# Attention fillers and attended tiles: the splits of four attended tiles ahead of the 13th block's softmax, and the fourth group of values ahead of pair 7's projection

## The chip, the cores and the metric

The kernel runs on one core of a Trainium2 chip. The metric is device time in microseconds (us) of one execution. A core has a matrix engine (TensorE, PE in the profile; its weight loads are PEld), a vector engine (DVE), a scalar engine (ACT), GpSimd (POOL) and a queue engine (SP) that issues transfers. Each engine works through its own list of instructions in the order in which the program was written, and semaphores hold an instruction until what it needs is there. Matrix products land in eight PSUM banks; everything else lies in SBUF, here mostly in 41 "pages" of 128 x 1024 float32.

## The reference, cut to what matters

Two layers of a decoder trunk: a short gated convolution with its feed-forward, then dilated attention with its feed-forward, then a last norm. The change lies in the attention of the second layer.

```python
def dilated_attention_mixer(h, w_qkv, w_out, rel_bias):
    qkv = (h @ w_qkv).reshape(bsz, seq, 3, N_HEADS, HEAD_DIM)      # seq 1024, 16 heads x 64
    q, k, v = qkv[:, :, 0], qkv[:, :, 1], qkv[:, :, 2]
    for window, dilation in ((128, 1), (512, 4), (2048, 16)):
        o, l = dilated_branch(q, k, v, rel_bias, window, dilation)   # banded softmax attention
    alpha = jax.nn.softmax(jnp.stack(lses, axis=0), axis=0)
    o = jnp.sum(alpha[..., None] * jnp.stack(outs, axis=0), axis=0)
    return o.reshape(bsz, seq, D_MODEL).astype(h.dtype) @ w_out

x = x + dilated_attention_mixer(rms_norm(x, mix_norm[1]), attn_w_qkv[0], attn_w_out[0], rel_bias)
```

## The kernel before, in words

All large products are made of float32 operands that are split into a high and a low part (`split`, L134 to L146): ACT copies the source into a rounded high part (L144), DVE subtracts it from the source for the low part (L145), and PE makes three matmuls of the parts (`product`, L372 to L374: high by high, high by low, low by high).

Attention runs in 17 slots, `slot(n, ...)` for n = 0 to 16. Slot n is what the change calls block n + 1, so the 13th block is slot 12. Slot n holds the scores of head n (`scores`, matmuls L1573 and L1574, DVE adds the bias on eviction, L1584 to L1615, and keeps a maximum `m`), GpSimd's maximum over the partitions (`partition_all_reduce`, L1627, from `m` to `mb`), the softmax of head n (`softmax`: five subtractions on DVE, L1635, five exponentials on ACT, L1636), and the values of head n - 1 (`values`, matmuls L1646; ACT takes the result out of two banks, L1669 and L1670). Up to slot 13 (`LAG`) a slot is "lagged": first all scores, then all values.

Between these PE gets filler work, 15 steps in each slot, from one generator, `fill()`: the groups of `FILL` in their order, then the first half of the output projection.

```python
            for kind, g in FILL[1:]:
                if kind == "qk":
                    yield from projections(g)
                else:
                    for j in range(2):
                        yield from value_tiles(g, j)
            yield from out_product(0, range(AO), first)
```

`projections(p)` makes keys (part 1) and queries (part 0) of head pair p, 36 steps, 32 of them with matmuls; `emit` then scales them on DVE (L1139, L1141), rounds them on ACT (L1144), takes the low part on DVE (L1147), and GpSimd's queue stores them (L1145, L1148). `value_tiles(g, j)` makes the values of two pairs, 40 steps for a group, 32 of them with matmuls (L1516 to L1518); ACT takes each tile out (L1521), GpSimd's queue stores it (L1525). `load_kq(n + 1)` at the start of slot n loads the next head's keys, queries and, for even heads, the values of the pair before (`load_values`, L1533 and L1535), all from SP's queue. Counted in steps of 15 a slot, the fillers before the output projection are steps 1 to 192, and its first step is the third last of slot 12.

The output projection's first half (`out_product(0, range(4), first)`) needs the attended tiles of pairs 0 to 3. They were stored to DRAM (`odram`) as they came. At slot 12 they are loaded back by SP (`load_attended`, L1796, tiles `oin`) and split into `first` (ACT L144 `w_hi<-oin`, DVE L145 `w_lo<-oin`) by the generator `halves()`, one tile a step. Where in slot 12 its steps are taken is set by the `hook` lines in the second loop of `slot`: that loop's step i = 3 has the softmax.

Of the kernel before, what the change touches and what calls it, by code (L numbers as in the profile page):

```python
# [46 lines left out]
SOFT = 4  # L47
# [1 line left out]
AO_WIDE = 5  # L49
AO = 4  # L50
LAG = 13
FILL = (("v", 0), ("v", 1), ("v", 2), ("qk", 6), ("qk", 7), ("v", 3))
DEEP_ORDER = (1, 2, 5, 6, 7, 3, 4)


# [44 lines left out]
def trunk(ctx: ExitStack, tc: tile.TileContext, x, gains_in, cwi, ck, cwo, wqkv, wo, relb,  # L100
# [8 lines left out]
    def page(name, dt=F32):  # L109
        return pages.tile([128, 1024], dt, name=name, tag="page", bufs=PAGES)  # L110
# [236 lines left out]
    add_units(QK, QK_PAIRS, lambda u, n: wqkv[(KT, 0)[n] + u])  # L347
    for kind, g in FILL:
        if kind == "v":
# [1114 lines left out]
    def load_bias(h):  # L1464
        t = scope["pool"].tile([128, L1 + L2], F32, name="bias", tag="bias", bufs=2)
        base = tables.offset + h * G3
        nc.sync.dma_start(t[:, 0:L1], bass.AP(tensor=tables.tensor, offset=base, ap=[[1, 8], [A1, 16], [1, L1]]))
        nc.sync.dma_start(t[:, L1:L1 + L2], bass.AP(tensor=tables.tensor, offset=base + G0,
                                                    ap=[[1, 32], [A2, 4], [1, L2]]))
        return t  # L1470
# [8 lines left out]
    def attention(norm, qk):  # L1479
# [58 lines left out]
        def load_kq(n):  # L1538

            p, a = divmod(n, 2)  # L1540
            k, q = qk.kq[p, 1], qk.kq[p, 0]
            rows = lambda t, r: bass.AP(t.tensor, t.offset + r * S, [[S, 64], [1, S]])
            n0, n1 = (slice(64 * i, 64 * i + 64) for i in (a, 1 - a))
            KS[n], QS[n] = page("ka", F32R), page("qa", F32R)
            nc.sync.dma_start(KS[n][n0].bitcast(F32), rows(k, 64 * a))
            nc.sync.dma_start(KS[n][n1].bitcast(F32), rows(k, 128 + 64 * a))
            if n <= LAG + 1 and n % 2 == 0 and n:
                load_values(p - 1)
            for m in (n0, n1):
                nc.sync.dma_start(QS[n][m].bitcast(F32), rows(q, 64 * a))  # L1550
            nc.sync.dma_start(qlo[a][n0].bitcast(F32), rows(q, 128 + 64 * a))

        def classes(n):

            KC[n] = page("kca", F32R)
            for h in range(2):
                nc.scalar.activation(KC[n][:, half(h)], view(KS[n], h * HALF, [[1, 4], [4, 128]]), AF.Copy)
                yield
# [80 lines left out]
        def values(p, a, st):  # L1639
            lf, lh, ld, lp = (st[n] for n in ("lf", "lh", "ld", "lp"))  # L1640
            acc = [bank(), bank()]
            kd = [[128, 4], [1, 32]]
            b1 = [[32, 16], [1, 8]]

            def mm(ih, off, dims, u, rhs, first=False, last=False):
                nc.tensor.matmul(view(acc[ih], off, dims), vx[:, u, 64 * a:64 * a + 128], rhs,  # L1646
                                 start=first, stop=last)

            for ih in range(2):
                for r4 in range(4):  # L1650
                    mm(ih, r4 * 32, kd, 8 + r4, view(lf, ih * HALF + r4 * 32, kd), first=r4 == 0)
                    if r4 % 2:
                        yield
            for r4 in range(4):
                mm(1, r4 * 32, kd, 12 + r4, view(lh, r4 * 32, kd))
                if r4 % 2:
                    yield
            for j in range(8):
                off = (j % 4) * 8
                mm(j // 4, off, b1, j, view(ld, blk(j), b1), last=False)  # L1660
                if j:
                    mm(j // 4, off, b1, j - 1, view(lp, blk(j), b1), last=j % 4 == 3)
                yield
            o, z = st["o"], st["z"]
            n0 = slice(64 * a, 64 * a + 64)
            z0 = slice(64 - 64 * a, 128 - 64 * a)
            for ih in range(2):
                s = slice(ih * HALF, (ih + 1) * HALF)
                nc.scalar.activation(z[n0, s], acc[ih][z0], AF.Ln)  # L1669
                nc.scalar.activation(o[n0, s], acc[ih][n0], AF.Copy)  # L1670
            yield

        def finish(p):

            o, z = OZ.pop(p)
            if p < NPAIR - 1:
                nc.scalar.activation(z, z, AF.Exp, scale=-1.0)
                put_off.append((p, o, z))
                return
                yield  # L1680

            acts[p] = page("o_hi", F32R), page("o_lo", F32R)

            def scaled(h):
                nc.vector.tensor_tensor(out=o[:, half(h)], in0=o[:, half(h)], in1=z[:, half(h)], op=ALU.mult)

            def parts(h):
                split(o[:, half(h)], [t[:, half(h)] for t in acts[p]])

            def rest():  # L1690
                parts(1)

            nc.scalar.activation(z[:, half(0)], z[:, half(0)], AF.Exp, scale=-1.0)
            scaled(0)
            parts(0)
            yield
            nc.scalar.activation(z[:, half(1)], z[:, half(1)], AF.Exp, scale=-1.0)
            scaled(1)
            yield
            last_part.append(rest)  # L1700
            yield
            ensure(ahead_ao + KT - AO_WIDE)
            ensure(ahead_ao + KT - AO_WIDE + 4)
            yield
# [11 lines left out]
        def slot(n, dense, ndense, late=0, hook=iter(())):  # L1716

            def other(k):
                for _ in range(k):
                    next(dense, None)  # L1720

            p, a = divmod(n, 2)
            if n < H:
                new = dict(bias=bias.pop(n))
                sc = scores(p, a, new)
            else:
                sc = iter(())
            if n + 1 < H:
                load_kq(n + 1)
                bias[n + 1] = load_bias(n + 1)  # L1730
            if n:
                q, b = divmod(n - 1, 2)
                if b == 0:
                    OZ[q] = page("o"), page("z")
                old = live.pop(n - 1)
                old.update(o=OZ[q][0], z=OZ[q][1])
                pv = values(q, b, old)
            else:
                pv = iter(())
            extra = later = iter(())  # L1740
            lagged = n <= LAG
            if n + 1 < H:
                later = classes(n + 1)
            if lagged and a and p:
                ending.append(finish(p - 1))
            used = 0
            if lagged:
                for i in range(8):
                    next(sc, None)
                    if n or i % 2:  # L1750
                        other(1)
                        used += 1
                    if a and ending and i == 0:
                        run(ending.pop())
                run(sc)
            else:
                if a == 0 and not late:
                    other(1)
                    used += 1
                for i in range(8):  # L1760
                    next(sc, None)
                    next(pv, None)
                    next(pv, None)
                    if i >= late and i % 2 == 0:
                        other(1)
                        used += 1
                run(sc)
                run(pv)
                if a == 0:
                    extra = finish(p - 1)  # L1770
                if a == 0 and n < H:
                    load_values(p)
            left = max(ndense - used, 0)
            for i in range(8):
                next(pv, None)
                next(pv, None)
                if i == (2 if n > LAG + 1 else 5):
                    attended()
                if not lagged and (i < FIN0 or i > SOFT):
                    next(extra, None)  # L1780
                if i in (1, 2):
                    next(later, None)
                if i == (3 if lagged else SOFT):
                    if n < H:
                        live[n] = new
                        run(softmax(new))
                if i >= SOFT:
                    next(hook, None)
                other(left * (i + 1) // 8 - left * i // 8)
            run(pv)  # L1790
            run(extra)
# [35 lines left out]
        def fill():  # L1827
            for kind, g in FILL[1:]:
                if kind == "qk":
# [12 lines left out]
        for n in range(H):  # L1842
            if n == LAG - 1:
                done.update(load_attended(range(AO)))
            hook = halves() if n == LAG - 1 else iter(())
# [49 lines left out]
    with tc.tile_pool(name="first", bufs=1) as scope["pool"]:  # L1895
# [5 lines left out]
        qk = QueryKey(norm)  # L1901
# [155 lines left out]
```

## Time and profile before

| | before |
|---|---|
| median of 3 runs | 2121.59 us (2120.86 to 2122.68) |
| the profiled execution | 2121.1 us, span of its trace 2119.3 us |
| PE busy | 2088.8 us, 99% |
| PEld busy | 1795.5 us, 85% |
| DVE busy | 1737.2 us, 82% |
| ACT busy | 1023.0 us, 48% |
| POOL busy | 236.5 us, 11% |
| mean granted TensorE clock | 0.997 |

The times in rows of the trace count from the span's start. A row of the timeline has the start, the time until the end of the last of its instructions, the engine, the line of the kernel, the operation, what it writes and reads, the count, and in brackets how long the engine stood idle before it and what it then waited for. A row of the windows has, for a stretch of the span, its length, each engine's busy time and count in it, the granted clock, the share of the transfer engines that were busy, and the rate.

### The profile page before, as it was taken

What the parts mean: (1) busy time and instruction counts of PE and PEld (TensorE: products, weight loads), DVE (VectorE), ACT (ScalarE), POOL (GpSimd) and SP (SyncE); (2) the same over time, 40 slices, a digit from 0 to 9 for tenths busy, and PEclk for the clock granted to TensorE, in tenths of its full rate; (3) what the DMA queues carried; (4) which work ended last, traced back from release to release, by engine and by line L of the source; (5) the groups of instructions that cost most, each with busy time, mean ns of one, the idle gap of its engine ahead of it and who ended that gap; (6) DMA issues with size and microseconds to landing.
All of it is one profiled execution on the core that took longest, in us unless ns stands there. A gap on an engine that the chain in (4) does not pass through costs nothing.

```text
span 2119.3 us, 30767 instructions
## 1 busy us (share of the span) xinstructions
PE 2088.8 (99%) x11006; PEld 1795.5 (85%) x11006; DVE 1737.2 (82%) x3255; ACT 1023.0 (48%) x1868; POOL 236.5 (11%) x337
## 2 busy tenths in 40 slices
PE   9999999999999999999999999899999999999998
PEld 7788888888888888887799999888788888888887
DVE  8898769988888888878967777786998888888876
ACT  7433427443444554446545555554544434456435
POOL 1000000110101000010322222111011001001000
PEclk9999999999999999999999999999999999999999
DMA  7322642333332576350867778855223323358432
GB/s 220 95 95 70 229 139 70 109 110 103 107 110 102 170 216 201 107 174 33 274 202 178 185 178 212 211 172 149 70 82 108 108 100 111 115 187 244 157 95 80
DMA packets 141527, 300.77 MB, mean 142 GB/s; under 512 B 48252, under 2 KB 54478, under 8 KB 141376
## 3 DMA queue, kind: packets, MB, share of 16 engines
q1 hardware_dynamic: 107488, 201.94, 32.3%
q0 software_dynamic: 26256, 82.18, 12.3%
q10 hardware_dynamic: 7632, 14.70, 1.8%
q8 instruction: 87, 1.43, 0.3%
q14 instruction: 64, 0.52, 0.1%
HBM read 208.49 MB, written 82.93 MB: 138 GB/s over the span
## 4 chain that ended last, share of the span: by engine, by line
PE 45%; DVE 5%; ACT 2%; issue 1%; POOL 1%; DMA 0%; SPq 0%; DVEq 0%; ACTq 0%; POOLq 0%
PE bank L572 8%; PE bank L570 8%; PE bank L571 8%; PE bank L1646 4%; PE bank L373 2%; PE bank L374 2%; PE bank L372 2%; PE bank L662 1%; PE bank L665 1%; PE bank L664 1%; PE bank L1516 1%; PE bank L1517 1%; PE bank L1518 1%; PE bank L1574 1%; PE bank L1573 1%
## 5 line engine op out<-in xcount | busy, mean ns | idle before, releaser
L572 PE MATMUL bank<-b,w 128*128 128x512 f32 x1952 | 760.9, 390 | 5.3 <-DVE w L145 5.0
L570 PE MATMUL bank<-b,w 128*128 128x512 f32 x1952 | 760.8, 390 | 3.5 <-ACT w L144 2.2
L571 PE MATMUL bank<-b,w 128*128 128x512 f32 x1952 | 760.4, 390 | 0.3 <-DVE b L881 0.3
L572 PEld LDWEIGHTS bank<-b,w 128*128 128x128 f32 x1952 | 366.4, 188 | 86.5 <-DVE w L145 10.4
L570 PEld LDWEIGHTS bank<-b,w 128*128 128x128 f32 x1952 | 366.6, 188 | 79.5 <-ACT w L144 3.1
L571 PEld LDWEIGHTS bank<-b,w 128*128 128x128 f32 x1952 | 366.6, 188 | 75.2 <-DVE b L881 1.4
L144 ACT ACTIVATE w<-combo 128x512 fp32r<-128x512 f32 (+2 forms) x488 | 249.7, 542 | 237.1 <-DVE combo L192 220.5
L145 DVE TENSOR_TENSOR w<-combo,w 128x512 fp32r<-128x512 f32 (+2 forms) x488 | 278.3, 584 | 37.8 <-ACT w L144 37.0
L576 ACT ACTIVATE part<-bank 128x512 f32<-128x512 f32 x186 | 110.9, 596 | 375.6 <-PE bank L572 375.2
L145 DVE TENSOR_TENSOR w<-raw,w 128x512 fp32r<-128x512 f32 (+2 forms) x342 | 189.9, 577 | 37.0 <-ACT w L144 37.0
L580 DVE TENSOR_TENSOR part<-part,bank 128x256 f32<-128x256 f32 (+1 forms) x366 | 171.9, 502 | 29.3 <-PE bank L572 16.6
L144 ACT ACTIVATE w<-raw 128x512 fp32r<-128x512 f32 (+2 forms) x342 | 167.3, 531 | 45.9 <-PE bank L572 12.2
L372 PE MATMUL bank<-w_hi,w 128*128 128x512 f32 (+1 forms) x400 | 151.1, 378 | 4.1 <-ACT w_hi L144 4.1
L373 PE MATMUL bank<-w_lo,w 128*128 128x512 f32 (+1 forms) x400 | 149.5, 374 | 1.5 <-DVE w_lo L145 1.5
L374 PE MATMUL bank<-w_hi,w 128*128 128x512 f32 (+1 forms) x400 | 149.5, 374 | 0.7 <-DVE w L145 0.7
L491 DVE TENSOR_TENSOR x<-x,bank 128x512 f32<-128x512 f32 (+1 forms) x104 | 66.5, 645 | 61.7 <-PE bank L374 60.8
L800 DVE TENSOR_TENSOR x<-x,bank 128x512 f32<-128x512 f32 x136 | 93.4, 687 | 28.2 <-PE bank L572 28.0
L192 DVE TENSOR_TENSOR combo<-raw 128x512 f32<-128x512 f32 (+1 forms) x172 | 111.8, 651 | 0.0
L372 PEld LDWEIGHTS bank<-w_hi,w 128*128 128x128 f32 x400 | 75.6, 189 | 17.0 <-ACT w_hi L144 4.5
L374 PEld LDWEIGHTS bank<-w_hi,w 128*128 128x128 f32 x400 | 75.5, 189 | 14.7 <-DVE w L145 1.6
L373 PEld LDWEIGHTS bank<-w_lo,w 128*128 128x128 f32 x400 | 75.7, 189 | 14.3 <-DVE w_lo L145 2.1
L563 DVE TENSOR_TENSOR b<-hin,b 128x512 fp32r<-128x512 f32 x126 | 79.7, 690 | 9.3 <-ACT b L562 9.2
(241 smaller groups left out, 3454.4 us busy)
## 6 DMA issues: line engine op xcount, KB each, us to landing
hin<-part SPq DMA_DIRECT2D x126, 256.0 KB
raw<-in_ffn_w_gate SPq DMA_DIRECT2D x44, 512.0 KB
raw<-in_ffn_w_up SPq DMA_DIRECT2D x44, 512.0 KB
part<-sum POOLq DMA_DIRECT2D x72, 256.0 KB, 2.3
raw<-in_ffn_w_down SPq DMA_DIRECT2D x48, 384.0 KB
raw<-in_attn_w_qkv SPq DMA_DIRECT2D x27, 512.0 KB
raw<-in_conv_w_in SPq DMA_DIRECT2D x24, 512.0 KB
part<-part POOLq DMA_DIRECT2D x36, 256.0 KB, 2.6
```

What stands on the lines that cost most here:

```text
L144: nc.scalar.activation(hi, src, AF.Copy)
L145: eng.tensor_tensor(out=lo, in0=src, in1=hi, op=ALU.subtract)
L192: eng.tensor_tensor(out=c, in0=a, in1=b, op=op)
L372: nc.tensor.matmul(b, whi[:, a], ahi[:, s], start=first, stop=False)
L373: nc.tensor.matmul(b, whi[:, a], alo[:, s], start=False, stop=False)
L374: nc.tensor.matmul(b, wlo[:, a], ahi[:, s], start=False, stop=last)
L570: nc.tensor.matmul(b, hi[:, a], bhi, start=start and k == 0, stop=False, skip_group_check=True)
L571: nc.tensor.matmul(b, hi[:, a], blo, start=False, stop=False, skip_group_check=True)
L572: nc.tensor.matmul(b, lo[:, a], bhi, start=False, stop=k == n - 1, skip_group_check=True)
L576: nc.scalar.activation(t, b, AF.Copy)
L580: nc.vector.tensor_tensor(out=t, in0=t, in1=b, op=ALU.add)
L800: nc.vector.tensor_tensor(out=X[n][:, half(h)], in0=X[n][:, half(h)], in1=b, op=ALU.add)
```

## The change

Two things. In `slot`, the steps of `hook` move from i = 4 to 7 of the second loop to i = 0 to 3, and stand ahead of the softmax in step 3: all four attended tiles are split before the softmax of slot 12. In `FILL`, the fourth group of values changes places with the projection of pair 7; the weights' loads and splits follow the same table.

```diff
-FILL = (("v", 0), ("v", 1), ("v", 2), ("qk", 6), ("qk", 7), ("v", 3))
+FILL = (("v", 0), ("v", 1), ("v", 2), ("qk", 6), ("v", 3), ("qk", 7))
...
                 if i in (1, 2):
                     next(later, None)
+                if i < 4:
+                    next(hook, None)
                 if i == (3 if lagged else SOFT):
                     if n < H:
                         live[n] = new
                         run(softmax(new))
-                if i >= SOFT:
-                    next(hook, None)
                 other(left * (i + 1) // 8 - left * i // 8)
```

On ACT, in slot 12, before: `kca` are the next head's keys by class, `lf` to `lp` the exponentials, `z` and `o` the values' results, `v` a tile of the fourth group of values.

```order
L1557 ACTIVATE kca<-ka 128x512 x2
L1636 ACTIVATE lf<-lf 128x1024
L1636 ACTIVATE lh<-lh 128x512
L1636 ACTIVATE ld<-ld 128x1024
L1636 ACTIVATE lp<-lp 128x16x24
L1636 ACTIVATE lp<-lp 128x512
L144 ACTIVATE w_hi<-oin 128x1024
L1521 ACTIVATE v<-bank,scales 128x256
L144 ACTIVATE w_hi<-oin 128x1024 x2
L1669 ACTIVATE z<-bank 64x512
L1670 ACTIVATE o<-bank 64x512
```

And on ACT in slot 12 now, where `kq_hi` is a part of pair 7's queries:

```order
L1144 ACTIVATE kq_hi<-kq 128x512
L144 ACTIVATE w_hi<-oin 128x1024
L1557 ACTIVATE kca<-ka 128x512
L144 ACTIVATE w_hi<-oin 128x1024
L1557 ACTIVATE kca<-ka 128x512
L144 ACTIVATE w_hi<-oin 128x1024 x2
L1636 ACTIVATE lf<-lf 128x1024
L1636 ACTIVATE lh<-lh 128x512
L1636 ACTIVATE ld<-ld 128x1024
L1636 ACTIVATE lp<-lp 128x16x24
L1636 ACTIVATE lp<-lp 128x512
L1144 ACTIVATE kq_hi<-kq 128x512
```

The four copies of the attended tiles now stand ahead of the five exponentials, between the copies of the keys; the last part of pair 7's queries has come behind the exponentials, ahead of the values' results.

On DVE, in slot 12, before: from the last two steps of the scores' maximum to the first eviction of slot 13's scores.

```order
L1623 TENSOR_TENSOR m<-m,ld 128x512
L1624 TENSOR_TENSOR m<-m,lp 128x512
L1635 TENSOR_TENSOR lf<-lf,mb 128x1024
L1635 TENSOR_TENSOR lh<-lh,mb 128x512
L1635 TENSOR_TENSOR ld<-ld,mb 128x1024
L1635 TENSOR_TENSOR lp<-lp,mb 128x16x24
L1635 TENSOR_TENSOR lp<-lp,mb 128x512
L145 TENSOR_TENSOR w_lo<-oin,w_hi 128x1024 x4
L1584 TENSOR_TENSOR lf<-bank,bias 128x4x64 x4
```

The same stretch of DVE now:

```order
L1623 TENSOR_TENSOR m<-m,ld 128x512
L1624 TENSOR_TENSOR m<-m,lp 128x512
L145 TENSOR_TENSOR w_lo<-oin,w_hi 128x1024 x4
L1635 TENSOR_TENSOR lf<-lf,mb 128x1024
L1635 TENSOR_TENSOR lh<-lh,mb 128x512
L1635 TENSOR_TENSOR ld<-ld,mb 128x1024
L1635 TENSOR_TENSOR lp<-lp,mb 128x16x24
L1635 TENSOR_TENSOR lp<-lp,mb 128x512
L1141 SCALAR_TENSOR_TENSOR kq<-bank,rstd 128x512
L1147 TENSOR_TENSOR kq_lo<-kq,kq_hi 128x512
L1584 TENSOR_TENSOR lf<-bank,bias 128x4x64 x4
```

The four subtractions for the low parts stand ahead of the softmax's five, directly behind the maximum that GpSimd reduces, and two instructions for pair 7's queries have come behind the softmax.

On GpSimd's queue, in slots 11 to 13 now (`ISA mb<-m` is the maximum over the partitions, first that of slot 11; `odram` the store of an attended tile, `kq_1` and `kq_0` the stores of pair 7's keys and queries):

```order
L1627 ISA mb<-m 128x1024
L1145 DMA kq_1_2930<-kq_hi 128x512
L1148 DMA kq_1_2930<-kq_lo 128x512
L1711 DMA odram_90<-o 128x1024
L1145 DMA kq_0_2929<-kq_hi 128x512
L1148 DMA kq_0_2929<-kq_lo 128x512
L1627 ISA mb<-m 128x1024
L1145 DMA kq_0_2929<-kq_hi 128x512
L1148 DMA kq_0_2929<-kq_lo 128x512
L1627 ISA mb<-m 128x1024
```

Before, the last stores in this place were those of the fourth group of values (`vdram`), ahead of the maximum of slot 13; now they are the last two stores of pair 7's queries, which `load_kq(14)` at the start of slot 13 reads back.

## The prediction

> **What bounds the kernel now.** The page's first part says that PE is the clock of this kernel:
>
> ```profile
> PE 2088.8 (99%) x11006; PEld 1795.5 (85%) x11006; DVE 1737.2 (82%) x3255; ACT 1023.0 (48%) x1868; POOL 236.5 (11%) x337
> ```
>
> With 99% busy, only two things can change the time: an idle stretch of PE, or a stretch in which it runs slowly. So I read the timeline of PE through all of attention for brackets, the only part that the change touches. From slot 4 on there are two places with brackets. The large one is the end of slot 12 and the start of slot 13:
>
> ```profile
> 1340.67 0.39 PE L1646 MATMUL bank<-ld,vx 128*128 128x128 f32 x2
> 1340.90 0.39 PE L1646 MATMUL bank<-lp,vx 128*128 128x128 f32 x2
> 1345.01 0.51 PE L372 MATMUL bank<-w_hi,w 128*128 128x512 f32 x1 [3.73 <-ACT w_hi L144]
> 1346.27 0.79 PE L373 MATMUL bank<-w_lo,w 128*128 128x512 f32 x1 [0.75 <-DVE w_lo L145]
> ...
> 1351.58 0.50 PE L372 MATMUL bank<-w_hi,w 128*128 128x512 f32 x1 [0.33 <-ACT w_hi L144]
> 1352.84 0.50 PE L373 MATMUL bank<-w_lo,w 128*128 128x512 f32 x1 [0.77 <-DVE w_lo L145]
> 1353.18 0.39 PE L374 MATMUL bank<-w_hi,w 128*128 128x512 f32 x1
> 1353.41 0.28 PE L1573 MATMUL bank<-qa,kca 128*128 128x256 f32 x1
> 1353.53 0.28 PE L1574 MATMUL bank<-ql,kca 128*128 128x256 f32 x1
> ```
>
> L372 to L374 with `w_hi` on the left are the first products of the output projection, and `w_hi`, `w_lo` are the attended tiles' parts. PE waits for them four times. Between two of the waits it is slow as well, in the window of 2 us (length, then PE, PEld, DVE, ACT, POOL; then the granted clock):
>
> ```profile
> 1346.00:1348.00 2.00, 1.73 (x6) 1.54 (x7) 1.92 (x3) 1.97 (x4) 1.79 (x4) 0.51 0.59 117
> ```
>
> The clock is 0.51 there, for 0.997 in the mean of the whole execution. Why the parts are late is seen on DVE, whose list has them behind the softmax:
>
> ```profile
> 1334.90 0.69 DVE L1624 TENSOR_TENSOR m<-m,lp 128x512 f32<-128x512 f32 x1
> 1339.02 1.23 DVE L1635 TENSOR_TENSOR lf<-lf,mb 128x1024 f32<-128x1024 f32 x1 [3.44 <-POOL mb L1627]
> ...
> 1341.90 1.16 DVE L1635 TENSOR_TENSOR lp<-lp,mb 128x384 f32<-128x384 f32 x2
> 1344.99 3.67 DVE L145 TENSOR_TENSOR w_lo<-oin,w_hi 128x1024 fp32r<-128x1024 f32 x3 [1.94 <-ACT w_hi L144]
> ```
>
> DVE stands idle for 3.44 us until GpSimd's maximum is there, runs the five subtractions from 1339.0 to 1343.1, idles 1.94 us more, and only then takes low parts. ACT's copies stand behind the exponentials in the same way.
>
> **Part 1: the splits ahead of the softmax.** What PE loses at this place: the last pair of values ahead of the gap starts at 1340.90, and these pairs follow each other in 0.23 us (1340.67 to 1340.90), so the next matmul was due at 1341.13. By 1353.41 PE has done four steps of the projection, 12 matmuls at 0.23 (1353.18 to 1353.41), 2.8 us; four pairs of values at 0.23, 0.9 us; and four score matmuls at 0.12 (1353.41 to 1353.53), 0.5 us. That is 4.2 us of work in 12.3 us: **8.1 us lost**, 5.6 of them in the four brackets, 2.5 by the slow pace.
>
> Would the parts be ready at 1341.1? The tile view gives both kinds of instruction, and the timeline of ACT the key copies that they now stand among:
>
> ```profile
> L144 ACT ACTIVATE w_hi<-oin x7: 1041/1044/1060, 1343.9 to 1416.3; 128x1024 fp32r<-128x1024 f32 x7
> L145 DVE TENSOR_TENSOR w_lo<-oin,w_hi x7: 1217/1224/1226, 1345.0 to 1417.7; 128x1024 fp32r<-128x1024 f32 x7
> ```
>
> ```profile
> 1333.26 2.16 ACT L1557 ACTIVATE kca<-ka 128x512 fp32r<-128x512 f32 x2
> ```
>
> ACT: four copies of 1.04 and the two key copies (2.16 together) are 6.3 us; even if the group starts only where the key copies start now, 1333.3, it ends at 1339.6, its first copy at 1334.3. DVE: the maximum's last step ends at 1335.6; two instructions for pair 7 join ahead of it and two weight splits of like size leave, so I leave it there, with 1 us of doubt.
>
> Then the four low parts meet GpSimd's maximum, which starts at that moment. What that does is shown where DVE had such work before. Rows of GpSimd, of DVE, and the line view of L1147 (min, median, max in ns):
>
> ```profile
> 1222.44 3.22 POOL L1627 PARTITION_ALL_REDUCE mb<-m  x1 [6.36 <-DVE m L1624]
> 1284.02 3.21 POOL L1627 PARTITION_ALL_REDUCE mb<-m  x1 [6.39 <-DVE m L1624]
> 1335.77 3.22 POOL L1627 PARTITION_ALL_REDUCE mb<-m  x1 [9.21 <-DVE m L1624]
> ...
> 1223.06 3.47 DVE L145 TENSOR_TENSOR w_lo<-raw,w_hi 128x1024 fp32r<-128x1024 f32 x2
> 1273.16 2.36 DVE L145 TENSOR_TENSOR w_lo<-raw,w_hi 128x1024 fp32r<-128x1024 f32 x2 [3.54 <-ACT w_hi L144]
> 1285.12 1.33 DVE L1147 TENSOR_TENSOR kq_lo<-kq,kq_hi 128x512 fp32r<-128x512 f32 x1 [0.70 <-ACT kq_hi L1144]
> L1147 DVE TENSOR_TENSOR kq_lo<-kq,kq_hi x32: 676/691/1333, 1012.8 to 1295.6; 128x512 fp32r<-128x512 f32 x32
> ```
>
> The `kq_lo` inside the maximum of 1284.02 took 1.33 for a median of 0.69, 0.64 more; the two splits inside that of 1222.44 took 3.47 for 2.36 outside, 1.11 more. Taken as a hold ahead of the work, the first was let go at 1285.76 and the second at 1224.17, both 1.7 us behind the maximum's start. So I count four low parts of 1.18 (2.36 for two) and one hold of 1.7: from 1335.8 + 1.7 = 1337.5 to 1342.2, ready at 1338.7, 1339.9, 1341.0 and 1342.2. PE needs the first at 1341.1, the second and third from 1342.7 on (a step 0.7, the values 0.9), the fourth at 1344.6. All four brackets go, and with them the slow pace: **-8.1 us**. The softmax, which started at 1339.0, starts at 1342.2 and ends at 1346.3.
>
> The Trainium skill, "SBUF — State Buffer", section "SBUF: two separate sides", calls the port pair of these two engines an exclusive lock: a DVE operation with two sources in SBUF and a GpSimd operation that reads SBUF block each other for the whole instruction. The trace agrees that DVE is held, but for 1.7 us of 3.2, not the whole. By the rule the low parts would end at 1343.7; that is rival (b).
>
> **Part 2: the swapped fillers.** Both groups have 32 steps with matmuls, so PE's work is the same. What moves is pair 7's scaling and storing, from slots 7 to 10 into slots 10 to 12, and the values' evictions the other way. The second place where PE idles lies in slot 10:
>
> ```profile
> 1287.27 1.23 DVE L1635 TENSOR_TENSOR lf<-lf,mb 128x1024 f32<-128x1024 f32 x1 [0.82 <-POOL mb L1627]
> ```
>
> ```profile
> 1287.68 0.28 PE L1573 MATMUL bank<-qa,kca 128*128 128x256 f32 x1
> ...
> 1293.41 0.38 PE L1573 MATMUL bank<-qa,ka 128*128 128x256 f32 x1 [1.14 <-ACT o L1670]
> ```
>
> PE waits 1.14 us for a bank that ACT frees behind slot 9's exponentials, and these are late because DVE first stood 3.54 us at a weight split of the next filler (1273.16, above), at slot 9's start. In the new order that double split is not there (slot 9's two come singly, later), so the softmax of slot 9 starts some us earlier: **-1.1 us**.
>
> The same chain could now form in slot 13, where pair 7's last two instructions on DVE and one on ACT stand between the softmax and the banks. There the softmax begins at 1342.2 and slot 13 on PE at 1341.1 + 3.0 = 1344.1, a lead of 1.9 us; in slot 10 the lead was 0.4 and PE lost 1.14. The extra `kq` work, three instructions near 0.7, eats the lead. So this costs between nothing and 1.14 in slot 13, and the same again in slot 14, whose softmax is late by the same amount: 0 to 2.3, I take **+1.5**, since the leads are near that of slot 10. A further gain is excluded, since PE has no other bracket in these slots to lose.
>
> Transfers: in slot 13 SP's queue stood for the fourth group's stores, which are early now; it stands for pair 7's last store instead, with bias, slabs and spilled tiles queued behind it, as before.
>
> **The sum.** -8.1 - 1.1 + 1.5 = -7.7 us, from the profiled execution's 2121.1 to 2113.4; its own time is 0.5 below the median, so in the median's terms 2121.6 - 7.7 = **2113.9 us**. A difference of 0.2%, 4.2 us, is about what a measurement of this kernel can tell from no change.
>
> **The rivals.**
>
> (a) SP's queue eats part of it. Rows of SP's queue (`oin` the loads of attended tiles) and of its waits (total, times, longest):
>
> ```profile
> 1311.87 1.88 SPq L1796 DMA_DIRECT2D oin<-odram  x4
> ...
> 1323.23 0.34 SPq L158 DMA_DIRECT2D raw<-in_attn_w_out  x1
> ...
> 1354.27 1.46 SPq L1550 DMA_DIRECT2D qa<-kq  x2
> SPq L1533 <- DMA vdram<-v: 12.4, 1, 12.4
> SPq L158 <- DMA oin<-odram: 2.0, 1, 2.0
> ```
>
> Before, the queries of head 14 were asked for at 1354.3, 18 us ahead of slot 14, which starts on PE here:
>
> ```profile
> 1372.41 0.28 PE L1573 MATMUL bank<-qa,kca 128*128 128x256 f32 x1
> ```
>
> Now they wait for pair 7's last low part, which leaves DVE at about 1348.2 (1346.3 and 1.9 for two instructions and ACT's rounding between them), and for its landing. If that takes as long as the slowest landing seen in this stretch (four tiles asked for by 1313.8, the last in by 1323.2, 9.5 us) they are asked for at 1357.7 and land as late as 1367.2, while slot 14 is due at 1364.3, 8.1 earlier than now (no bracket stands between 1353.41 and 1372.41). That gives back 2.9 us: 2113.9 + 2.9 = 2116.8. Against it: the 9.5 us were four tiles in one row, these are three smaller ones. Chance 0.12.
>
> (b) GpSimd and DVE hold each other longer. Either the hold lasts as long as the maximum, to 1339.0, or the low parts, which follow the maximum's last step without a gap, keep GpSimd out until all four are done, at 1340.3 (1335.6 and 4.7), and the maximum ends 3.2 later. The softmax then starts at 1343.7 or 1343.5, 1.5 later than counted; with both bank waits in full, 2.3, and this 1.5 on top, the change is -8.1 - 1.1 + 3.8 = -5.4: 2116.2. Against it: the two holds of 1.7 us above; for it: none of those low parts started ahead of its maximum. Chance 0.15.
>
> (c) Slower: the attended tiles come too late. The projection of pair 7 reads both halves of the layer's input up to step 192, so pages that were free in slot 11 are held longer, and the four loads may stand in SP's queue for them. Before, the four were in at 1323.2. Wanted are the copies' sources at 1333.3, and PE is hurt when the first copy starts later than about 1339. Before, the first copy started at 1343.9 and PE lost 8.1 us, so a start at 1343.9 gives 2113.9 + 8.1 = 2122.0, and each further us costs one, with the softmax and slot 13's evictions queued behind: from a start at 1347.7 on the time is over 2125.8. The loads would have to land 25 us later than before (pages of slot 11's products come free when these are done, before slot 12's values and so well before 1340). Chance 0.06.
>
> (d) The change does nothing: the parts are early, but slot 13 then waits for the softmax or its loads as long as it waited for them. DVE's work from 1335.6 to the end of slot 13's maximum would have to fill the time; it was idle 3.44 and 1.94 us in slot 12 alone, so not. 2121.6; chance 0.04.
>
> **How the numbers follow.** My forecast, 2111.4 to 2115.7 by the bounds of the small terms (nothing or 2.3 for 1.5) and 1 us of doubt on the large one, has 0.63. Faster by over 0.2% are the forecast, (a) and (b) but for 0.03 in which both come together: 0.87. Within 0.2%: (d) and that 0.03, 0.07. Slower: (c), 0.06. The range goes from 2111.0, a little under the forecast's lower end, to 2118.0, which takes in (a) and (b) and leaves out about 0.15.
>
> **What would show it.** Right: no bracket at the first products of the output projection, the clock at 1.00 through 1340 to 1350, `w_lo<-oin` beside GpSimd's maximum and held by less than 2 us, the score matmuls of 1353.41 at about 1345.3 and slot 14 at about 1364.3. Part 2 shows as no bracket in slot 10. Wrong: new brackets of PE in slots 13 or 14 behind `o L1670`, `lf L1584` or a load, an `oin` that lands after 1336, or a first low part after 1341.

## The result, and the profile after

The changed kernel takes 2112.36 us (median of 4 runs, 2111.99 to 2113.60), before 2121.91 (4 runs, 2120.86 to 2122.68): a ratio of 0.9957, 95% interval 0.9945 to 0.9968. That is 9.5 us faster; forecast were 7.7. A second set of 5 runs gave 2112.91 us and 0.9959 (0.9945 to 0.9972).

PE is as busy as it was, in a span that is 7.5 us shorter (2111.8 for 2119.3), in the page's first part:

```profile
PE 2088.2 (99%) x11006; PEld 1796.4 (85%) x11006; DVE 1737.2 (82%) x3255; ACT 1021.1 (48%) x1868; POOL 236.8 (11%) x337
```

The timeline of PE after, at the first two of the four products that had brackets before, and then the starts of slots 8, 13 (its second class of scores), 14 and 15:

```profile
1341.12 0.48 PE L372 MATMUL bank<-w_hi,w 128*128 128x512 f32 x1
1341.43 0.39 PE L373 MATMUL bank<-w_lo,w 128*128 128x512 f32 x1
...
1251.12 0.29 PE L1573 MATMUL bank<-qa,kca 128*128 128x256 f32 x1
1345.35 0.28 PE L1573 MATMUL bank<-qa,kca 128*128 128x256 f32 x1
1364.71 0.28 PE L1573 MATMUL bank<-qa,kca 128*128 128x256 f32 x1
1384.98 0.28 PE L1573 MATMUL bank<-qa,kca 128*128 128x256 f32 x1
```

No bracket stands at the output projection, nor anywhere from slot 4 to the last slot. The clock, 0.51 in the window of 1346 to 1348 before, is 1.00 there now, and 1.00 over the whole of 1340 to 1350 (the window of 2 us after: length, then PE, PEld, DVE, ACT, POOL, the granted clock, and transfers):

```profile
1346.00:1348.00 2.00, 2.00 (x14) 1.78 (x14) 1.30 (x3) 2.00 (x4) 0.00 (x0) 1.00 0.87 173
```

On the other engines the parts now stand ahead of the softmax (timelines of ACT, GpSimd and DVE after, and the tile view of the low parts):

```profile
1331.45 1.05 ACT L144 ACTIVATE w_hi<-oin 128x1024 fp32r<-128x1024 f32 x1
1336.69 4.05 POOL L1627 PARTITION_ALL_REDUCE mb<-m  x1 [1.86 <-DVE m L1624]
1336.43 6.32 DVE L145 TENSOR_TENSOR w_lo<-oin,w_hi 128x1024 fp32r<-128x1024 f32 x4
1342.68 1.21 DVE L1635 TENSOR_TENSOR lf<-lf,mb 128x1024 f32<-128x1024 f32 x1
```

```profile
L145 DVE TENSOR_TENSOR w_lo<-oin,w_hi x7: 1210/1218/2914, 1336.4 to 1410.3; 128x1024 fp32r<-128x1024 f32 x7
```

The first copy starts at 1331.45 instead of 1343.9. The four low parts fill 1336.43 to 1342.75, the first of them with 2.91 us where 1.22 is the median. Absolute times of the two executions can't be set side by side: slot 8 starts 2.1 us later in this one (1251.12 for 1249.00), from differences ahead of it. Lengths can. From slot 8's start to slot 15's, before and after (timeline of PE before):

```profile
1249.00 0.28 PE L1573 MATMUL bank<-qa,kca 128*128 128x256 f32 x1
...
1392.40 0.28 PE L1573 MATMUL bank<-qa,kca 128*128 128x256 f32 x1
```

that is 143.40 us before and 133.86 after (1384.98 less 1251.12), **9.54 less**, as much as the whole gain of the medians. The second profiled execution of the same kernel had 133.86 again, so this length tells more than the time of one run.

### The profile page after: what moved, and what is told of

Read it like the earlier page. It is cut to its first block, busy times and chain, and to the rows that moved or that the text cites. A ratio compares the mean times of both kernels' runs of the same rounds, so it can differ in the third digit from the quotient of the medians.

```text
span 2111.8 us, 30764 instructions
## 1 busy us (share of the span) xinstructions
PE 2088.2 (99%) x11006; PEld 1796.4 (85%) x11006; DVE 1737.2 (82%) x3255; ACT 1021.1 (48%) x1868; POOL 236.8 (11%) x337
```

## The experiments

The kernels were timed in three sets, each on a chip of its own and with the kernel before beside them; that one had 2121.63, 2121.55 and 2121.32 us in the three, so medians of different sets can differ by some 0.3 us for the chip alone. The lengths are read from each profile as differences of the slots' first score matmuls: slot 12, slot 13, and slots 8 to 14 together.

| kernel | median us (runs) | slot 12 | slot 13 | slots 8 to 14 |
|---|---|---|---|---|
| before | 2121.6 (27) | 24.79 | 21.81 | 143.40 |
| the splits alone | 2117.23 (11) | 18.29 | 22.98 | 138.02 |
| the fillers alone | 2121.82 (11) | 27.10 | 21.34 | 142.72 |
| both (the change) | 2112.91 (5) | 18.76 | 20.51 | 133.86 |
| splits, values taken out earlier | 2112.76 (5) | 18.29 | 20.20 | 135.15 |
| the same, double weight split apart | 2112.23 (5) | 18.29 | 20.19 | 134.20 |
| change, one subtraction more | 2113.32 (5) | 18.76 | 21.79 | 135.17 |
| change, three subtractions more | 2117.77 (11) | 18.76 | 26.94 | 139.98 |
| change, two of four splits behind | 2117.67 (11) | 23.62 | 21.88 | 139.78 |

**The two halves alone.** The splits alone, against the changed kernel:

```diff
-FILL = (("v", 0), ("v", 1), ("v", 2), ("qk", 6), ("v", 3), ("qk", 7))
+FILL = (("v", 0), ("v", 1), ("v", 2), ("qk", 6), ("qk", 7), ("v", 3))
```

> The splits ahead of the softmax, the fillers in the old order. Theory (the two parts of the change are worth what they are worth alone): the gap of slot 12 goes, -8.1, the wait of slot 10 stays: 2121.9 - 8.1 = 2113.8 us, with 1.1 idle in slot 10 behind ACT o, the first product of the output projection without a bracket, and no slow clock in slot 12. Rival (the swap is needed too, since the values' evictions and stores of slots 11 and 12 stand among the splits): a bracket is left at the first products, 2116 us or more.

It took 2117.23 us, ratio 0.998 (0.9971 to 0.9989), which is the rival's time, but by neither's mechanism. The bracket at the first products is gone as the theory has it, but a new one stands in slot 13, at another place than the rival's (timelines of PE, ACT, GpSimd and SP's queue, and as the last row GpSimd's of the kernel before):

```profile
1325.36 0.29 PE L1573 MATMUL bank<-qa,kca 128*128 128x256 f32 x1
1344.83 0.28 PE L1573 MATMUL bank<-qa,kca 128*128 128x256 f32 x1
1355.68 1.58 PE L1646 MATMUL bank<-lf,vx 128*128 128x128 f32 x12 [2.55 <-DMA vx<-vdram]
1346.18 0.45 ACT L1521 ACTIVATE v<-bank,scales 128x256 f32<-128x256 f32 x1
1346.92 2.17 POOL L1525 DMA_DIRECT2D vdram<-v  x4 [7.58 <-ACT v L1521]
1351.59 0.38 SPq L1533 DMA_DIRECT2D vx<-vdram  x1
...
1345.62 2.17 POOL L1525 DMA_DIRECT2D vdram<-v  x4 [6.62 <-ACT v L1521]
```

From slot 12's start to the score matmuls that the prediction marked PE takes 19.47 us (the first two rows), for 27.60 before (1325.81 to 1353.41): 8.13 less, the whole gap. But the last tile of the fourth group of values stands on ACT behind slot 12's exponentials: it is taken out at 1346.2, stored from 1346.9 and loaded as `vx` from 1351.6. Before it was stored only 1.3 us earlier (from 1345.62), and PE, which came to these values 8 us later, never noticed. Now it waits 2.55 us.

The fillers alone, against the kernel before:

```diff
-FILL = (("v", 0), ("v", 1), ("v", 2), ("qk", 6), ("qk", 7), ("v", 3))
+FILL = (("v", 0), ("v", 1), ("v", 2), ("qk", 6), ("v", 3), ("qk", 7))
```

> The fillers in the new order, the splits behind the softmax as before. Theory: the wait of slot 10 goes, -1.1, and the gap of slot 12 stays as it was (3.73 + 0.75 + 0.33 + 0.77 idle, clock 0.51 behind it): 2120.8 us, 2120.0 to 2121.4. Rival (the swap did most of it): 2117 us or less. Second rival (pair 7's last parts stand ahead of the splits on ACT and DVE and make the gap longer): above 2121.9.

It took 2121.82 us, ratio 1.000 (0.9991 to 1.0009): no gain, where the theory had 1.1. Slot 10's wait is gone, but the gap in slot 12 grew (timeline of PE, and the window behind the gap):

```profile
1343.31 0.50 PE L372 MATMUL bank<-w_hi,w 128*128 128x512 f32 x1 [4.60 <-ACT w_hi L144]
1344.58 0.79 PE L373 MATMUL bank<-w_lo,w 128*128 128x512 f32 x1 [0.76 <-DVE w_lo L145]
...
1351.64 0.50 PE L373 MATMUL bank<-w_lo,w 128*128 128x512 f32 x1 [0.58 <-DVE w_lo L145]
```

```profile
1345.00:1347.00 2.00, 2.00 (x9) 1.81 (x9) 2.00 (x4) 1.76 (x3) 0.55 (x1) 0.50 0.04 9
```

Counted from slot 8's start, PE reaches the gap 2.0 us earlier and the first high part comes only 1.2 us earlier, so PE waits 4.60 for 3.73. Pair 7's parts, which the second rival blamed, do not cause this wait: ACT makes the first two copies directly behind the exponentials (from 1342.22). In the length of slots 8 to 14 0.68 us of gain are left, in the median nothing. So the swap is worth nothing by itself and 4.3 us on top of the splits (2117.23 to 2112.91), and the splits 4.4 by themselves and 8.9 on top of the swap (2121.82 to 2112.91).

**Is it the values' transfer?** The splits alone, with the softmax of slot 12 written behind the filler step that takes the last tile out:

```diff
-                if i == (3 if lagged else SOFT):
+                if i == ((5 if n == LAG - 1 else 3) if lagged else SOFT):
```

> The splits ahead of the softmax, the old order of the fillers, and the softmax of slot 12 written two steps later, which changes one thing: on ACT the last tile of values (v) is taken out ahead of the exponentials instead of behind them, so that its store and the load of vx behind it start about 7 us earlier. Theory (what the splits alone lacked was this transfer): no wait for vx in slot 13, and as only slot 10's wait (1.15) is left over the changed kernel, 2112.4 + 1.2 = 2113.6 us, 2113.0 to 2114.2. Rival (SP's queue stands there for another transfer, the spilled tiles or a page): a bracket at the first values of slot 13 of 1 us or more, 2115.5 us or more.

It took 2112.76 us, ratio 0.9961 (0.9947 to 0.9974), 0.2 under the theory's range, and the wait for `vx` is gone as the theory has it. One eviction on ACT, seven us earlier, gives back nearly all that the splits alone lacked (the timelines again):

```profile
1339.37 0.47 ACT L1521 ACTIVATE v<-bank,scales 128x256 f32<-128x256 f32 x1 [0.30 <-PE bank L1518]
1340.14 2.17 POOL L1525 DMA_DIRECT2D vdram<-v  x4 [0.50 <-ACT v L1521]
1346.37 0.38 SPq L1533 DMA_DIRECT2D vx<-vdram  x1
1293.27 0.39 PE L1573 MATMUL bank<-qa,ka 128*128 128x256 f32 x1 [1.14 <-ACT o L1670]
```

The last row, in slot 10, is the only bracket left from slot 4 on. The two profiled executions took 2115.22 and 2112.76 us, 2.46 apart, about the wait (slots 8 to 14 differ by 2.87); the medians differ by 4.47. The runs of the splits alone spread from 2115.1 to 2119.5, and the profiled one was the second fastest. Five of the eight runs above 2116 have a mean clock of 0.996 for its 0.998, so there is a slow stretch in them, behind this wait or in slot 3; none of them was profiled.

**Where slot 10's wait comes from.** As that kernel, with the double weight split at slot 9's start taken apart (in `projections`):

```diff
-                w = take(("qkv", p, part), 2 - part)
+                w = take(("qkv", p, part), 1 if p == 7 else 2 - part)
...
+                    ensure(op_state[1] + (p == 7 and part == 0 and h == 1))
                     b = bank()
```

> As the kernel with the earlier values, and the double weight split ahead of the fourth group of values (on ACT and DVE at slot 9's start) taken apart: one stays, the other moves to slot 9's second loop, beside GpSimd's maximum. Theory (slot 10's wait comes from that double split, and the swap of the fillers is worth these two waits and nothing more): no bracket in slot 10, DVE's idle time at slot 9's start near 2.5 instead of 3.5 us, 2112.4 us, as the changed kernel. Rival (the wait has another source, or the swap has a worth of its own): slot 10's bracket stays and the time is that of the kernel before, 2113.6 us.

It took 2112.23 us, ratio 0.9959 (0.9946 to 0.9971), with slots 8 to 14 in 134.20. The rows of DVE, GpSimd and PE:

```profile
1276.15 1.22 DVE L145 TENSOR_TENSOR w_lo<-raw,w_hi 128x1024 fp32r<-128x1024 f32 x1 [3.52 <-ACT w_hi L144]
1285.83 3.21 POOL L1627 PARTITION_ALL_REDUCE mb<-m  x1 [6.35 <-issue]
1286.18 2.61 DVE L145 TENSOR_TENSOR w_lo<-raw,w_hi 128x1024 fp32r<-128x1024 f32 x1
1295.44 0.39 PE L1573 MATMUL bank<-qa,ka 128*128 128x256 f32 x1 [0.43 <-ACT o L1670]
```

The theory holds in part. The wait falls from 1.14 to 0.43, since slot 9's softmax now starts 1.10 ahead of slot 10 (1289.31 for 1290.41) instead of 0.41. DVE's idle time stayed at 3.52, where 2.5 was expected, since it ends with the first copy, which ACT still makes behind the values' results. And some 0.2 of the wait that is left comes from the edit: the subtraction that moved is held beside the maximum and keeps DVE busy until 1289.31, 0.27 behind the maximum's end.

**How much room slot 13 has.** The changed kernel with k subtractions more on DVE behind the fourth low part (k = 1 and 3; the source tile is dead by then). Measured from the first low part's start, the softmax starts 1.25 and 3.77 us later with them, where 1.14 and 3.42 were counted:

```diff
                 first[q] = split(t)
+                if q == AO - 1:
+                    for _ in range(k):
+                        nc.vector.tensor_tensor(out=t, in0=t, in1=first[q][0], op=ALU.subtract)
                 yield
```

> The changed kernel with one more subtraction of 128x1024 on DVE behind the fourth low part (in place in the dead source tile), so that slot 12's softmax starts 1.14 us later, at 1343.8. Theory now (in slot 13 the bank that PE needs at 1349.30 comes free at 1349.39, so nothing is left to spare): PE waits 1.2 us there and the time is 1.1 over the changed kernel's, 2113.4 us. Theory of the prediction (slot 13 and slot 14 each pay): 2.3 over, 2114.6 us. Rival (spare time is left): 2112.4 us.

> The changed kernel with three more subtractions, softmax 3.42 us later. Theory now: PE waits 3.5 us in slot 13, once, and the time is 3.4 over the changed kernel's, 2115.8 us, up to 2 more if the clock falls behind the wait. Theory of the prediction (both slots pay): 6.8 over, 2119.2 us. Rival (1 to 2 us to spare): 1.4 to 2.4 over, 2114 to 2115 us.

One more: 2113.32 us, ratio 0.9959 (0.9947 to 0.9972), slots 8 to 14 longer by 1.31, with 1.00 us of waiting in slot 13 (timeline of PE):

```profile
1347.02 0.39 PE L1573 MATMUL bank<-qa,ka 128*128 128x256 f32 x1 [0.35 <-DVE kq L1141]
1349.11 0.38 PE L1573 MATMUL bank<-qa,ka 128*128 128x256 f32 x1 [0.65 <-ACT o L1670]
```

Three more: 2117.77 us, ratio 0.9978 (0.9969 to 0.9986), 4.9 over the changed kernel; the timeline of PE and the window behind it:

```profile
1351.24 0.38 PE L1573 MATMUL bank<-qa,ka 128*128 128x256 f32 x1 [2.88 <-DVE kq L1141]
1353.34 0.58 PE L1573 MATMUL bank<-qa,ka 128*128 128x256 f32 x1 [0.58 <-ACT o L1670]
```

```profile
1353.00:1355.00 2.00, 1.67 (x6) 1.57 (x7) 2.00 (x6) 1.93 (x4) 0.55 (x1) 0.50 0.69 262
```

PE waits 3.46 us, as the theory after the result had it, in one slot and not in two. In this execution, the slowest of eleven, slots 8 to 14 are 6.12 longer, and the clock of 0.50 accounts for nearly all of the rest. By the lengths there is no room: a softmax 1.25 us later costs 1.31. The medians show it only for the three subtractions; with one more, the ratio to the kernel before is 0.9959, as that of the changed kernel.

**Two splits ahead are not enough.**

```diff
-                if i < 4:
+                if 2 <= i < 6:
                     next(hook, None)
```

> The changed kernel with two of the four attended tiles split ahead of the softmax and two behind it. Theory: the softmax starts at 1340.7 instead of 1342.7 and its exponentials end at 1345.6, so the third high part is there at 1346.6 while PE wants it at 1343.5: 3.1 idle there, 0.9 more at its low part, and up to 2.5 for a halved clock behind them: 2116.4 to 2118.9 us. Rival (two parts ahead are enough, since PE has work for the time): 2113 us or less.

It took 2117.67 us, ratio 0.9983 (0.9974 to 0.9991), as the theory has it, with the first wait to the tenth (3.11 for 3.1) and the second half as long as expected (0.46 for 0.9; timeline of PE and a window):

```profile
1345.23 0.80 PE L372 MATMUL bank<-w_hi,w 128*128 128x512 f32 x1 [3.11 <-ACT w_hi L144]
1346.49 0.79 PE L373 MATMUL bank<-w_lo,w 128*128 128x512 f32 x1 [0.46 <-DVE w_lo L145]
```

```profile
1346.00:1348.00 2.00, 1.54 (x6) 1.32 (x6) 2.00 (x3) 0.97 (x3) 0.00 (x0) 0.50 0.72 147
```

**The stall that is left, and a faster kernel.** The changed kernel still waits in slot 3 (timeline of PE):

```profile
1159.94 0.38 PE L1573 MATMUL bank<-qa,ka 128*128 128x256 f32 x1 [1.07 <-ACT o L1670]
1161.17 0.48 PE L1573 MATMUL bank<-qa,ka 128*128 128x256 f32 x1 [0.51 <-ACT o L1670]
```

It is slot 10's chain: two weight splits hold DVE at slot 2's start, and the softmax that follows is late for slot 3. Against the changed kernel, in `value_tiles`:

```diff
-                if j and b4 in (1, 2):
-                    ensure(op_state[1] + b4 - 1)
+                if j and b4 in ((0, 1) if g == 1 else (1, 2)):
+                    ensure(op_state[1] + b4 - (g != 1))
```

> The changed kernel with the two weight splits for the third group of values one step of the filler loop's eight earlier: of the two on DVE in slot 2 (1138.1 and 1141.9), which hold its first evictions, one moves into slot 1. Theory (the same chain as in slot 10: late evictions, late maximum, late softmax, late bank): slot 2's softmax starts about 2 us earlier, the waits of slot 3 go (1.07 + 0.51, and the slow stretch behind them; slot 3 takes 18.4 instead of 21 to 22 us), 2112.4 - 2.7 = 2109.7 us, 2109.0 to 2110.2. Rival (the wait moves to slot 2, whose softmax comes later by the split): 2112.4 us. Second rival (the banks in slot 3 are late for another reason): waits as before, 2112.4 us.

It took 2110.39 us, ratio 0.9947 (0.9934 to 0.9959). Slot 3 fell from 21.97 to 18.35 us, and slot 2 grew from 18.34 to 19.39: both theory and first rival have a share, since this bracket is new:

```profile
1140.76 0.38 PE L1573 MATMUL bank<-qa,ka 128*128 128x256 f32 x1 [0.49 <-ACT o L1670]
```

Beside the changed kernel on one chip, and against a version that keeps the second split in slot 2 but behind its first evictions (`(1, 3)` for `(0, 1)`):

> The changed kernel as it is, beside the two versions of slot 2's weight splits on the same chip. All theories: 2112.4 us, 2111.9 to 2113.6.

> The version with one weight split moved from slot 2 into slot 1, once more, beside the changed kernel. Theory: slot 3's waits (2.7 us with their slow stretch) gone, slot 2's wait of 0.49 new, so 1.5 to 2.5 under the changed kernel: 2110.4 us. Rival (the first comparison was of two chips): no difference.

> The changed kernel with the second of the two weight splits that hold DVE in slot 2 moved later within slot 2, behind the evictions of its first scores, in place of one moved into slot 1. Theory: DVE no longer idles 1.86 us for it, so slot 2's maximum starts 1.9 earlier (1148.5 in the changed kernel's time), the softmax has a lead of about 1.8 us on slot 3 and all waits of slots 2 and 3 go: 2112.4 - 2.7 = 2109.7 us. Rival (the lead is too small): a wait of 0.1 to 0.5 left in slot 3, 2110.4 us.

They took 2112.91 us, 2110.41 (ratio 0.9949, 0.9936 to 0.9961) and 2110.75 (0.9951, 0.9939 to 0.9964). The first version is about 2.5 us faster than the change again. The other leaves a wait in slot 3, as its rival said (0.33, behind `v L1521`; slot 3 takes 19.05). The intervals against before overlap; the slots do not: slots 2 and 3 together take 37.7, 37.4 and 40.5 us in the three (moved, later, changed).

## Why the prediction was right, and where not

**The gap, -8.1: right.** All four brackets and the slow clock went, and with the old fillers that stretch is 8.13 shorter (19.47 for 27.60). The high parts started at 1331.45 (counted on by 1334.3), the low parts were done at 1342.75 (1342.2).

**The hold of GpSimd on DVE: right in size.** The first low part took 1.70 over the median, against 1.7 counted, and in the kernel with the double split apart the one beside the maximum of 1285.83 ended at 1288.8, 1.7 and a usual 1.2 behind the maximum's start. Of rival (b) one thing came true: the first low part did start ahead of the maximum (1336.43 and 1336.69), and the maximum took 4.05 instead of 3.22, not the 3.2 more that the rival had. It ended at 1340.7, ahead of the low parts, and cost nothing. The softmax came 0.5 later than counted because the low parts started at 1336.4, not 1335.6.

**Slot 10, -1.1: right.** The bracket went. No split stands at slot 9's start on DVE any more, and slot 9's softmax starts 4.16 ahead of slot 10 (1283.61 for 1287.77) instead of 0.41. The experiment took only one of the two splits from there, left DVE's idle time as it was, and left 0.43 of the wait; what that idle time is worth alone was not tested.

**The bank waits, +1.5: the term that was mis-sized.** In slot 13 it measured 0.15: PE was due at 1349.30 (the last product of 1349.07, and 0.23) and started at 1349.45 (timelines of PE and DVE after).

```profile
1349.07 0.40 PE L374 MATMUL bank<-w_hi,w 128*128 128x512 f32 x1
1349.45 0.39 PE L1573 MATMUL bank<-qa,ka 128*128 128x256 f32 x1
1361.81 1.23 DVE L1635 TENSOR_TENSOR lf<-lf,mb 128x1024 f32<-128x1024 f32 x1 [2.83 <-POOL mb L1627]
```

The step set slot 10's 1.14 against the leads of the softmax and the `kq` work alone. Slot 13 has one product more (0.7) ahead of that bank, its lead was 1.5 for 0.4, and ACT has one copy more (0.6) ahead of the results. Counted by starts, as the 0.15 is, slot 10's wait was 1.30 (due at 1292.11, started at 1293.41), and 1.30 - 0.7 - 1.1 + 0.6 is 0.1. That slot 14 would pay the same again was wrong as well. Its softmax is later: it starts 2.90 ahead of slot 14 (1361.81 for 1364.71), for 5.22 before (1367.19 for 1372.41). But 2.90 is enough for no bracket to stand there; the slot takes 0.28 more than before (20.27 for 19.99), for a reason that stays open. The mechanism is there, as the two kernels with a later softmax show; only at this place it hardly bit yet.

**The sum: short by 1.8.** Slots 8 to 14 gained 9.54 for 7.7 forecast; 1.1 of that is the bank term (0.15 and 0.28 for 1.5), 0.2 is slot 10 (1.29 in lengths for 1.1), and the rest, some 0.6, is not put down to a place. That 1345.3 and 1364.3 were met within 0.4 us is partly luck, since slot 8 was 2.1 us later in this execution.

**What the swap is worth: the step that failed.** Part 2 gave it 1.1 and had the early stores of the fourth group as a change without a price. Alone it is worth nothing in the median, because the gap takes up most of what PE gains ahead of it; with the splits it is worth 4.3. In the lengths of slots 8 to 14 that is 4.16 us, of which 2.87 are the wait for `vx` that the splits alone bring up (138.02 to 135.15) and 1.29 slot 10. Nor is the swap the only way to that gain: with the last tile of values taken out earlier, the splits reach 2112.76 us without it. The total was near because both parts were made at once.

**The rivals.** (a) fell: the queries of head 14 were asked for at 1351.5, not 1357.7, and no bracket stands at slot 14. (c) fell, though its ground was there: the four loads stood 6.76 us in SP's queue and were issued up to 1322.2, still 9 us ahead of the first copy. (d) fell.

```profile
1315.41 6.76 SPq L1796 DMA_DIRECT2D oin<-odram  x4
1351.51 2.09 SPq L1550 DMA_DIRECT2D qa<-kq  x2
```

## What to carry to other kernels

Price a stall together with the next thing that is late behind it: work moved ahead of a softmax makes everything queued behind that softmax later, and one eviction there (0.45 us on ACT) cost the kernel with the splits alone 2.9 us in the length of its slots and 4.5 in the median. Ahead of a long stall a gain on the bound engine is worth nothing, and it becomes worth something when the stall goes, so parts of a change should be timed alone and together. Where runs spread by several us, the length of the slots between two fixed matmuls tells kernels apart that medians can't.

## What the runs showed of the hardware

A wait can cost more than its length. The granted clock was 0.50 to 0.51 behind waits of 4.60, 3.73, 3.11 and 2.88 us, each of which had a second one of 0.46 to 0.76 close behind it. It was 1.00 behind the one of 2.55, which stood alone and was seen in one execution (the window of the splits alone):

```profile
1356.00:1358.00 2.00, 2.00 (x19) 1.92 (x18) 0.00 (x0) 0.00 (x0) 2.00 (x1) 1.00 1.19 258
```

In slot 3 the clock was 0.50 behind two short waits (1.07 and 0.51) in the changed kernel's execution, and 1.00 behind such waits in that of before. Of the ten profiled executions that have these waits it fell in three, those of the change and of the change with three subtractions, where slot 3 took 22.0 to 22.1 us, and in the other seven it stayed and the slot took 21.0 to 21.1 (window of after, then the timeline and the window of before):

```profile
1162.00:1164.00 2.00, 2.00 (x12) 2.00 (x11) 1.47 (x4) 2.00 (x4) 0.00 (x0) 0.50 0.26 77
```

```profile
1158.78 0.39 PE L1573 MATMUL bank<-qa,ka 128*128 128x256 f32 x1 [1.10 <-ACT o L1670]
1160.02 0.38 PE L1573 MATMUL bank<-qa,ka 128*128 128x256 f32 x1 [0.49 <-ACT o L1670]
```

```profile
1162.00:1164.00 2.00, 2.00 (x18) 2.00 (x19) 1.76 (x6) 1.85 (x2) 0.00 (x0) 1.00 0.21 33
```

The Trainium skill, "TensorE: Matmul & The Clock Gate", section "What's actually happening", says that the clock is set by activity in a window of about 3.4 us that runs freely. That like waits sometimes halve it and sometimes don't agrees with this; that waits well under 3.4 us can suffice is what the traces add.

Beside the maximum DVE was held only where both sources lay in SBUF, and only until about 1.7 us behind the maximum's start. An addition with one source in a PSUM bank ran beside it at its usual 0.68 (timelines of DVE and GpSimd after):

```profile
1358.30 0.68 DVE L491 TENSOR_TENSOR x<-x,bank 128x512 f32<-128x512 f32 x1
1358.56 3.21 POOL L1627 PARTITION_ALL_REDUCE mb<-m  x1 [8.82 <-DVE m L1624]
```

The maximum itself took 4.04 to 4.05 in all eleven traces in which a low part had started on DVE 0.26 us ahead of it, whether four followed each other or two. It stayed at 3.21 to 3.22 where low parts started behind it: 0.35 behind in the row of 1285.83, and 0.62 behind in the prediction's rows of 1222.44 and 1223.06, two in a row. So the order of the starts goes with the longer maximum, not the number of low parts; why stays open.
